# SwiGLU FFN of a two-layer decoder trunk: more products ahead of the operand combinations, and the last pair's two matrices in turns

## The chip, the cores and the metric

One Trainium2 chip, one core. The metric is the device time of one execution in microseconds, lower is better; for the kernel before it is the median of three runs.

## What is computed

A decoder trunk of two layers over 1024 tokens of width 1024, in float32. Layer 0 mixes tokens with stick-breaking and sliding-window attention, layer 1 with multi-head latent attention. Each layer ends in the part that the change touches, and both layers run it alike:

```python
def swiglu(h, w_gate, w_up, w_down):            # 1024 -> 2816 -> 1024
    return (jax.nn.silu(h @ w_gate) * (h @ w_up)) @ w_down

for layer in range(DEPTH):
    ...
    h = rmsnorm(x, ffn_norm[layer])
    x = x + swiglu(h, ffn_w_gate[layer], ffn_w_up[layer], ffn_w_down[layer])
return rmsnorm(x, final_norm)
```

## The kernel before

Activations lie transposed: a tile is 128 features by 512 tokens (half A or half B of the tokens). Every float32 operand is split in two float32r parts: ACT rounds it to the high part, DVE subtracts to get the low part. `split_w` (lines 141 to 147) does it for weights (tiles whi, wlo), `split` (lines 914 to 916) for activations. `mm3` (lines 228 to 232) then makes three matmuls: high by high, high weight by low activation, low weight by high activation.

The FFN (`ffn`, line 918) multiplies blocks two by two in Winograd's way: seven products in place of eight. The hidden width is taken as 11 pairs of 128-wide blocks. For each pair and for each of the two matrices (gate, g = 0; up, g = 1) there are seven products, named after the activation operand that they use, the *form*: B11, B21, T2, T1, T3, B22, N4. A form is four tiles (k = 0 to 3), each split in high and low. One product is 12 matmuls of 128x512 on PE. Four PSUM names take turns for the results (mm, a, b, d). On the weight side a matrix is loaded as four blocks (wa, wa, wb, wb); POOL makes three sums and differences of them and a fourth later (`combine` and `prep` in `forms`, lines 171 to 224). `take` prepares weights four products ahead of the one that is issued.

The FFN has three stages:

- **The head.** Forms B11 and B21 need half A alone, which is normalised first. So for the first NA = 4 pairs the products B11 and B21 of both matrices come first (16 products, lines 996 to 1014); their sums are written to DRAM (`keep`) and fetched again later. Meanwhile `combinations(k)` (line 984) makes the five other forms from half B: two normalised tiles (h_tile, line 950), one DVE and three POOL subtractions, five splits. It is called once at the end of each of the four pairs, for k = 0 to 3.
- **The pairs.** For each of the 11 pairs gate, then up: the remaining five products for the first four pairs (weights of kind "rest", which need all four POOL operations before their first product), all seven for the others (kind "fast", whose first two products need none). DVE adds the products up, ACT applies SiLU to gate, DVE multiplies by it, and `combine` (line 959) makes the four combined operands for the down projection on POOL. All go to DRAM. In layer 0 POOL also computes rotary tables in this stage (`rope_tables`), one step after each product.
- **Down.** The down projection takes the pairs in chunks of 4, 4 and 3. Its seven forms for a chunk are fetched from DRAM and split by `build` (line 1061) into the same tiles that the forms of the stage before used, so a tile can be written only when its last product has read it. For the first chunk the 28 tiles are fetched through a ring of three tiles named lone, after all pairs; for the next chunks, form by form behind the products of the last column of the chunk before.

Each engine has one queue that runs in order. The order in it is laid out at build time by a scheduler that follows the program's order and its own estimate of when each operand is ready.

Of the kernel before, what the change touches and what calls it, by code (L numbers as in the profile page):

```python
# [10 lines left out]
F32 = mybir.dt.float32  # L11
# [3 lines left out]
AF = mybir.ActivationFunctionType  # L15
ALU = mybir.AluOpType
# [55 lines left out]
class Kernel:  # L72
# [98 lines left out]
    def forms(self, mats):  # L171
# [7 lines left out]
        flat = [(i, j) for i, m in enumerate(mats) for j in range(len(turns.get(m[0], m[1])))]  # L179
        raws, ready = {}, []  # L180

        def load(i):
# [6 lines left out]
            if kind != "plain":  # L189
                t.append(self.tl(self.wx, [P, HALF], F32, "s1"))  # L190
# [8 lines left out]
        def prep():  # L199
            i, j = flat[len(ready)]  # L200
            kind, _, n = mats[i]
            if j == 0:
                for x in (i, i + 1):
                    if x < len(mats) and x not in raws:
                        load(x)
# [712 lines left out]
    def ffn(self, layer, xt, rs, accs, first, last):  # L918
# [13 lines left out]
        NA = 4  # L932
# [14 lines left out]
        take = self.forms(mats)  # L947
# [48 lines left out]
        tb = ExitStack()  # L996
        for i in range(NA):
            for g in range(2):
# [14 lines left out]
                elif g == 1:  # L1013
                    combinations(i)
# [3 lines left out]
        with self.pool("tc", side="right") as self.tp:  # L1018
            t = lambda tag: self.tl(self.tp, [P, HALF], F32, tag)
            for i in range(NP):  # L1020
# [3 lines left out]
                for g in range(2):  # L1024

                    def done(x, key, name=None):
                        if g == 0:
                            nc.scalar.activation(x, x, AF.Silu)
                            sil[key] = x
                        else:  # L1030
                            nc.vector.tensor_tensor(x, x, sil[key], ALU.mult)  # L1031
                            if name:
                                keep(x, name, i)

                    u, c11 = t(f"u{g}"), t(f"c11{g}")
                    if i < NA:
                        fetch(u, f"U{g}", i)
                        if g == 0:
                            sil[0] = c11
                        else:  # L1040
                            fetch(c11, "B11", i)
                    else:
                        nc.scalar.copy(u, p("B11"))
                        add(c11, u, p("B21"))
                        done(c11, 0, "B11")
                    add(u, u, p("T2"))
                    p5, c12, c22 = p("T1"), t(f"c12{g}"), t(f"c22{g}")
                    add(c12, u, p5)
                    add(u, u, p("T3"))
                    add(c22, u, p5)  # L1050
                    done(c22, 1, "B22")
                    add(c12, c12, p("B22"))
                    done(c12, 2)
                    add(u, u, p("N4"))
                    done(u, 3, "B21")
                combine(i, c11, c12, u, c22, sil[0], sil[2], sil[1])
            for _ in side:
                pass
# [7 lines left out]
            for name in FORMS:  # L1066
                build(name, *chunks[0], (self.rp, [P, HALF], F32, "lone", 3))
# [604 lines left out]
```

## Time and profile before

| | |
|---|---|
| time, median of 3 runs (lowest to highest) | 2510.03 us (2509.27 to 2511.41) |
| time of the profiled execution | 2502.03 us |
| its span, first to last instruction | 2500.3 us |
| PE busy (matmul) | 2334.6 us, 93% |
| DVE busy | 1912.7 us, 77% |
| ACT busy | 1237.0 us, 49% |
| POOL busy | 979.4 us, 39% |
| mean granted TensorE clock | 0.972 |
| HBM traffic | 115 GB/s over the span |

The busy shares are averages over stages with different limits. Views by stretch, engine by engine, tell more: a view of windows gives for each stretch the busy time and number of instructions of each engine, and a timeline lists instructions with the idle time ahead of each and what ended it.

### The profile page before, as it was taken

The page shows a single profiled execution, that of the slowest core. Times are in us where ns is not written, and L with a number is a line of the kernel's source. Part 1 is how long each engine was busy: PE and PEld are TensorE (multiplying, and loading weights), DVE is VectorE, ACT ScalarE, POOL GpSimd, SP SyncE. Part 2 cuts the span into 40 slices and gives each one's busy share as a digit, 9 for nine tenths or more (in the row PEclk, how much of TensorE's full clock was granted, in tenths as well). Part 3 has the DMA queues.
Part 4 walks back from the last instruction along what each step waited for, and adds up shares of the span by engine and source line. Part 5 has one row for each costly group of instructions (what it writes and reads, how often), then busy time and mean ns, then how long its engine had stood idle before and what let it go on. Part 6 is the DMA issues. An engine that isn't in the chain of part 4 may idle for free. (4 is left out here: it accounts for less than half of the span.)

```text
span 2500.3 us, 33743 instructions
## 1 busy us (share of the span) xinstructions
PE 2334.6 (93%) x11252; PEld 1913.9 (77%) x11252; DVE 1912.7 (77%) x2864; ACT 1237.0 (49%) x2469; POOL 979.4 (39%) x786
## 2 busy tenths in 40 slices
PE   7999999888999999899987999999989999998996
PEld 4777787776788888678766888887768888886784
DVE  6777776779676667799977888885588766678988
ACT  5555555554233334344655787774453333343453
POOL 5333232216975354343222323321047544533333
PEclk9999999999999999999998999999989999999998
DMA  3011225543444234453333111135225433345531
GB/s 119 26 43 39 68 99 192 189 171 122 141 137 140 88 107 151 145 171 123 121 115 95 50 62 60 53 133 195 90 96 183 146 105 102 107 129 170 169 103 71
DMA packets 161931, 289.22 MB, mean 116 GB/s; under 512 B 20091, under 2 KB 28764, under 8 KB 161756
## 3 DMA queue, kind: packets, MB, share of 16 engines
q1 hardware_dynamic: 161756, 287.05, 35.1%
q8 instruction: 89, 1.46, 0.2%
q14 instruction: 86, 0.70, 0.1%
HBM read 207.19 MB, written 79.27 MB: 115 GB/s over the span
## 5 line engine op out<-in xcount | busy, mean ns | idle before, releaser
L145 ACT CAST whi<-wa 128x512 fp32r<-128x512 f32 (+1 forms) x422 | 255.8, 607 | 473.3 <-PE mm L231 118.8
L146 DVE TENSOR_TENSOR wlo<-wa,whi 128x512 fp32r<-128x512 f32 (+1 forms) x422 | 334.0, 792 | 63.9 <-ACT whi L145 62.2
L177 POOL TENSOR_TENSOR wa<-s,wa 128x512 f32<-128x512 f32 (+1 forms) x68 | 97.0, 1426 | 327.1 <-DVE wlo L146 297.8
L195 POOL TENSOR_TENSOR s<-wb,wb 128x512 f32<-128x512 f32 (+1 forms) x68 | 104.6, 1538 | 161.6 <-DVE wlo L146 146.2
L146 DVE TENSOR_TENSOR wlo<-wb,whi 128x512 fp32r<-128x512 f32 (+1 forms) x136 | 136.2, 1001 | 33.3 <-ACT whi L145 33.2
L1424 PE MATMUL z<-mk,mq 128*128 128x512 f32 (+2 forms) x576 | 148.1, 369 | 11.2 <-ACT w L1437 10.4
L145 ACT CAST whi<-wb 128x512 fp32r<-128x512 f32 (+1 forms) x136 | 82.3, 605 | 142.3 <-PE a L231 43.6
L230 PE MATMUL mm<-hh,whi 128*128 128x512 f32 x312 | 129.0, 413 | 1.7 <-ACT whi L145 1.7
L1437 ACT ACTIVATE w<-z,st 128x512 f32<-128x512 f32 (+3 forms) x192 | 110.9, 583 | 35.3 <-DVE st L1433 25.4
L231 PE MATMUL mm<-hl,whi 128*128 128x512 f32 x312 | 125.6, 403 | 0.0
L177 POOL TENSOR_TENSOR wa<-wa,wa 128x512 f32<-128x512 f32 (+1 forms) x68 | 100.0, 1471 | 65.3 <-issue 52.0
L232 PE MATMUL mm<-hh,wlo 128*128 128x512 f32 x312 | 125.4, 402 | 0.0
L1430 DVE TENSOR_REDUCE st<-z 128x1 f32<-128x512 f32 (+1 forms) x192 | 104.2, 550 | 26.8 <-PE z L1424 19.1
L391 DVE TENSOR_TENSOR ptl<-t,pth 128x512 fp32r<-128x512 f32 x160 | 108.2, 684 | 18.2 <-ACT pth L390 13.5
L927 POOL TENSOR_TENSOR c<-c,c 128x512 f32<-128x512 f32 x66 | 99.3, 1518 | 43.1 <-DVE c L1031 37.1
L1424 PEld LDWEIGHTS z<-mk,mq 128*128 128x128 f32 x576 | 93.4, 194 | 24.7 <-ACT w L1437 16.2
L177 POOL TENSOR_TENSOR wb<-wa,wb 128x512 f32<-128x512 f32 (+1 forms) x68 | 101.9, 1499 | 3.5
L390 ACT CAST pth<-t 128x512 fp32r<-128x512 f32 x160 | 91.1, 590 | 19.0 <-PE t L387 8.0
L395 PE MATMUL mm<-pth,v 128*128 128x256 f32 x320 | 94.6, 312 | 2.9 <-ACT pth L390 2.8
L387 PE MATMUL t<-ident,w 128*128 128x128 f32 x576 | 94.8, 277 | 1.3 <-ACT w L1437 1.2
L395 PE MATMUL mm<-ptl,v 128*128 128x256 f32 x320 | 88.0, 299 | 2.0 <-DVE ptl L391 2.0
L703 DVE TENSOR_TENSOR ptl<-t,pth 128x512 fp32r<-128x512 f32 x80 | 54.4, 683 | 41.0 <-ACT pth L702 40.5
(526 smaller groups left out, 7640.4 us busy)
## 6 DMA issues: line engine op xcount, KB each, us to landing
a<-c SPq DMA_DIRECT2D x124, 256.0 KB, 2.1
ld<-a SPq DMA_DIRECT2D x98, 256.0 KB, 3.7
wa<-w_gate SPq DMA_DIRECT2D x60, 256.0 KB, 2.7
wa<-w_up SPq DMA_DIRECT2D x60, 256.0 KB, 2.6
lone<-a SPq DMA_DIRECT2D x56, 256.0 KB, 3.3
wb<-w_gate SPq DMA_DIRECT2D x44, 256.0 KB, 2.9
wb<-w_up SPq DMA_DIRECT2D x44, 256.0 KB, 2.8
wa<-w_in SPq DMA_DIRECT2D x36, 256.0 KB, 2.6
```

Source lines behind the costliest of these rows:

```text
L145: nc.scalar.copy(hi[:, :n], raw[:, :n])
L146: nc.vector.tensor_tensor(lo[:, :n], raw[:, :n], f(hi[:, :n]), ALU.subtract)
L177: sub = lambda o, x, y: nc.gpsimd.tensor_tensor(o, x, y, ALU.subtract)
L195: nc.gpsimd.tensor_tensor(s1, a21, a22, ALU.add)
L230: mm(ps, wh, xh, start=first, stop=False)
L231: mm(ps, wh, xl, start=False, stop=False)
L232: mm(ps, wl, xh, start=False, stop=last)
L391: nc.vector.tensor_tensor(lo, t, f(hi), ALU.subtract)
L395: nc.tensor.matmul(o[:, :256], vs, pt[:, j * 256:(j + 1) * 256], start=(kb == kb0 and j == 0 and i == 0), stop=(kb == NB - 2 and j == 1 an ...
L1424: nc.tensor.matmul(z[:, :wd + ext], qq[:, q0:q0 + P], kk[:, k0 - ext:k0 + wd], start=y == 0, stop=y == 2 and x > 0)
L1430: nc.vector.tensor_reduce(st[:, x:x + 1], zs[x], AX.X, ALU.max, negate=True)
L1437: nc.scalar.activation(w[:, o:o + wd], zs[x], AF.Exp, bias=st[:, 2 * np_ - 2:2 * np_ - 1], accum_out=box[p]["s"][c // 2][:, 8 * x + j:8 * ...
```

## The change

It changes `forms` and `ffn` in three ways.

1. NA goes from 4 to 6: the head has 24 products, and two more pairs have their B11 sums written to DRAM and fetched.
2. `combinations(k)` becomes a generator of five parts; the 20 parts of the four k are taken one after each product of the head, from the third product on.
3. In the last pair gate and up take turns form by form (`twins`), and the first down chunk's operands of a form are built as soon as both matrices have used that form. For this both matrices' weights are held at once; the one extra weight tile (s1) of the second is taken from the ring lone, which `build` also uses. The first down matrix is loaded at the second matrix's last form instead of its first.

The core of the diff (the body of `outputs` is the old code with a `yield` after each product, and is cut here):

```diff
-    def forms(self, mats):
+    def forms(self, mats, twins=None):
...
+        if twins is not None:
+            both = [x for x in flat if x[0] in twins]
+            at = flat.index(both[0])
+            flat[at:at + len(both)] = sorted(both, key=lambda x: (x[1], x[0]))
...
-                t.append(self.tl(self.wx, [P, HALF], F32, "s1"))
+                t.append(self.tl(self.rp, [P, HALF], F32, "lone", 3) if twins is not None and i == twins[1] else
+                         self.tl(self.wx, [P, HALF], F32, "s1"))
...
-            if j == 0:
+            early = twins is not None and i == twins[1]
+            if j == (6 if early else 0):
                 for x in (i, i + 1):
                     if x < len(mats) and x not in raws:
                         load(x)
...
-        NA = 4
+        NA = 6
...
-        take = self.forms(mats)
+        twins = (2 * NA + 2 * NP - 2, 2 * NA + 2 * NP - 1)
+        take = self.forms(mats, twins)
...
-            h12, h22 = h_tile(k, B, t()), h_tile(4 + k, B, t())
-            t1, t2, n4 = t(), t(), t()
+            h12 = h_tile(k, B, t())
+            t1 = t()
             sub(t1, h12, raw["B11"][k])
+            yield
+            h22 = h_tile(4 + k, B, t())
+            part("B22", h22)
+            yield
+            t2 = t()
             sub(t2, h22, t1)
             nc.vector.tensor_tensor(h12, h22, h12, ALU.subtract)
+            part("T1", t1)
+            yield
+            n4 = t()
             sub(n4, raw["B21"][k], t2)
-            for n, x in (("T2", t2), ("T1", t1), ("T3", h12), ("B22", h22), ("N4", n4)):
-                F[n][k] = self.form_tile(n, k)
-                self.split(x, F[n][k])
+            part("T2", t2)
+            yield
+            part("T3", h12)
+            part("N4", n4)
+            yield
...
-                elif g == 1:
-                    combinations(i)
+                    side = (x for k in range(4) for x in combinations(k))
+        for _ in side:
+            pass
...
+                gs = [outputs(i, g, sil) for g in range(2)]
+                if i < NP - 1:
+                    for g in gs:
+                        for _ in g:
+                            pass
+                else:
+                    for n, name in enumerate(FORMS):
+                        for g in gs:
+                            next(g, None)
+                        if n > 0:
+                            build(FORMS[n - 1], *chunks[0], ring)
...
-            for name in FORMS:
-                build(name, *chunks[0], (self.rp, [P, HALF], F32, "lone", 3))
+            build(FORMS[-1], *chunks[0], ring)
```

How the built order changes, at two places of DVE's queue. The first is the head of layer 0, from the low part of the weights of product 10 to that of product 11; hb are the tiles of half B from which the forms are made. Before:

```order
L146 TENSOR_TENSOR wlo_5893<-wa_5791,whi_5892 128x512
L990 TENSOR_TENSOR hb_5813<-hb_5815,hb_5813 128x512
L916 TENSOR_TENSOR B22l_5837<-hb_5815,B22h_5836 128x512
L916 TENSOR_TENSOR T1l_5829<-hb_5817,T1h_5828 128x512
L950 SCALAR_TENSOR_TENSOR hb_5936<-x_11344_5239,gains_66,rr_5750 128x512
L950 SCALAR_TENSOR_TENSOR hb_5938<-x_11348_5247,gains_66,rr_5750 128x512
L916 TENSOR_TENSOR T2l_5825<-hb_5818,T2h_5824 128x512
L916 TENSOR_TENSOR T3l_5833<-hb_5813,T3h_5832 128x512
L146 TENSOR_TENSOR wlo_5917<-wa_5867,whi_5916 128x512
```

Of the change, the same place:

```order
L146 TENSOR_TENSOR wlo_5885<-wa_5795,whi_5884 128x512
L1008 TENSOR_TENSOR hb_5785<-hb_5813,hb_5785 128x512
L923 TENSOR_TENSOR B22l_5816<-hb_5813,B22h_5815 128x512
L923 TENSOR_TENSOR T1l_5846<-hb_5787,T1h_5845 128x512
L958 SCALAR_TENSOR_TENSOR hb_5932<-x_11344_5239,gains_66,rr_5750 128x512
L923 TENSOR_TENSOR T2l_5876<-hb_5842,T2h_5875 128x512
L923 TENSOR_TENSOR T3l_5901<-hb_5785,T3h_5900 128x512
L146 TENSOR_TENSOR wlo_5917<-wa_5853,whi_5916 128x512
```

One normalised tile of seven instructions has moved from between the two weight splits to behind them. The second place is the end of the pairs in layer 0, where the first down operands (B11l) enter DVE's queue. Before, among the products of the last up matrix:

```order
L928 TENSOR_TENSOR u_9223<-u_9223,d_9352 128x512
L146 TENSOR_TENSOR wlo_9375<-s_9145,whi_9374 128x512
L916 TENSOR_TENSOR B11l_9538<-lone_9539,B11h_9537 128x512
L916 TENSOR_TENSOR B11l_9544<-lone_9545,B11h_9543 128x512
L916 TENSOR_TENSOR B11l_9550<-lone_9551,B11h_9549 128x512
L146 TENSOR_TENSOR wlo_9393<-wb_9141,whi_9392 128x512
L916 TENSOR_TENSOR B11l_9556<-lone_9557,B11h_9555 128x512
L928 TENSOR_TENSOR c_9372<-u_9371,a_9391 128x512
```

Of the change, after the second of the last pair's 14 products:

```order
L1052 TENSOR_TENSOR u_9095<-u_9095,u_8947 128x512
L146 TENSOR_TENSOR wlo_9289<-wa_9025,whi_9288 128x512
L923 TENSOR_TENSOR B11l_9346<-lone_9347,B11h_9345 128x512
L923 TENSOR_TENSOR B11l_9352<-lone_9353,B11h_9351 128x512
L146 TENSOR_TENSOR wlo_9307<-wa_9175,whi_9306 128x512
L935 TENSOR_TENSOR c_9262<-u_9261,d_9305 128x512
L923 TENSOR_TENSOR B11l_9358<-lone_9359,B11h_9357 128x512
L146 TENSOR_TENSOR wlo_9326<-s_9033,whi_9325 128x512
L923 TENSOR_TENSOR B11l_9364<-lone_9365,B11h_9363 128x512
```

The first B11l stood behind the last pair's eighth product (the first of its up matrix) and stands behind the second now, with splits of weights and sums of products between the builds.

## Rows read from the trace of the kernel before

**Rows 1.** Windows of the core: length, busy us and instructions per engine, granted clock, DMA

```profile
core 0: us, PE busy (x) PEld busy (x) DVE busy (x) ACT busy (x) POOL busy (x), PEclk, DMA share, GB/s
570.00:610.00 40.00, 30.51 (x112) 23.86 (x111) 38.85 (x43) 19.99 (x35) 27.58 (x15) 0.87 0.28 89
1840.00:1870.00 30.00, 21.84 (x74) 16.72 (x74) 28.85 (x31) 13.71 (x25) 23.01 (x12) 0.83 0.23 79
1000.00:1030.00 30.00, 23.56 (x72) 14.78 (x71) 23.39 (x31) 12.77 (x22) 11.15 (x8) 0.83 0.70 228
2250.00:2290.00 40.00, 32.91 (x122) 23.55 (x121) 34.69 (x46) 16.19 (x28) 15.91 (x10) 0.91 0.73 235
1880.00:1970.00 90.00, 90.00 (x399) 74.47 (x398) 72.54 (x85) 26.04 (x45) 60.01 (x41) 1.00 0.53 178
620.00:710.00 90.00, 86.68 (x372) 70.28 (x371) 58.64 (x74) 22.69 (x39) 86.56 (x102) 0.98 0.44 145
1832.90:1877.00 44.10, 35.94 (x135) 27.96 (x134) 42.95 (x49) 21.57 (x37) 30.69 (x16) 0.88 0.31 104
1375.00:1687.00 312.00, 305.62 (x2037) 262.19 (x2036) 259.48 (x513) 246.93 (x638) 101.75 (x79) 1.00 0.22 71
```

**Rows 2.** Timeline of PE, head of layer 1: start, duration, idle before and its end

```profile
1838.69 0.39 PE L230 MATMUL mm<-B21h,whi 128*128 128x512 f32 x1
...
1841.41 0.39 PE L230 MATMUL a<-B11h,whi 128*128 128x512 f32 x1
...
1846.44 0.79 PE L232 MATMUL a<-B11h,wlo 128*128 128x512 f32 x1 [4.41 <-DVE wlo L146]
...
1857.27 0.80 PE L230 MATMUL a<-B11h,whi 128*128 128x512 f32 x1 [3.08 <-ACT whi L145]
```

**Rows 3.** Timeline of DVE, the same stretch

```profile
1832.90 1.41 DVE L950 SCALAR_TENSOR_TENSOR hb<-x,gains,rr 128x512 f32<-128x512 f32 x2
...
1835.94 1.77 DVE L990 TENSOR_TENSOR hb<-hb,hb 128x512 f32<-128x512 f32 x1
...
1839.35 0.68 DVE L916 TENSOR_TENSOR T1l<-hb,T1h 128x512 fp32r<-128x512 f32 x1
...
1844.64 1.74 DVE L146 TENSOR_TENSOR wlo<-wa,whi 128x512 fp32r<-128x512 f32 x1
...
1876.28 0.69 DVE L916 TENSOR_TENSOR T3l<-hb,T3h 128x512 fp32r<-128x512 f32 x1
```

**Rows 4.** Timeline of POOL, the same stretch, and one operation after it

```profile
1835.54 1.62 POOL L927 TENSOR_TENSOR hb<-hb,hb 128x512 f32<-128x512 f32 x1
...
1850.80 5.25 POOL L927 TENSOR_TENSOR hb<-hb,T1l 128x512 f32<-128x512 f32 x1 [4.96 <-DVE hb L950]
...
1887.91 1.29 POOL L195 TENSOR_TENSOR s<-wb,wb 128x512 f32<-128x512 f32 x1 [4.05 <-DMA wb<-w_gate]
```

**Rows 5.** Timelines of PE and ACT, end of the pairs in layer 1: last pair, eighth product

```profile
2227.89 0.39 PE L230 MATMUL b<-B11h,whi 128*128 128x512 f32 x1
...
2228.77 0.62 ACT L915 CAST B11h<-lone 128x512 fp32r<-128x512 f32 x1 [0.23 <-PE b L232]
```

**Rows 6.** Timelines of PE and DVE, first down column of layer 1

```profile
2257.03 0.50 PE L232 MATMUL mm<-T1h,wlo 128*128 128x512 f32 x1 [1.33 <-DVE wlo L146]
2261.61 0.50 PE L231 MATMUL mm<-T1l,whi 128*128 128x512 f32 x1 [2.47 <-DVE T1l L916]
...
2279.74 1.02 DVE L916 TENSOR_TENSOR N4l<-lone,N4h 128x512 fp32r<-128x512 f32 x1 [0.67 <-ACT N4h L915]
```

**Rows 7.** Tile lone, 2225 to 2285: idle of its users, and its transfers

```profile
  DMA lone<-a: 25.6, 22
...
DMA to landing us min/median/max: 2.6/2.9/3.4
```

**Rows 8.** Timeline of PE, pairs of layer 0

```profile
678.35 0.50 PE L232 MATMUL b<-T2h,wlo 128*128 128x512 f32 x1 [2.08 <-DVE wlo L146]
```

More of the change, by code (lines that the diff above doesn't have):

```diff
@@ L1019, in ffn, with outputs, done, build @@
             t = lambda tag: self.tl(self.tp, [P, HALF], F32, tag)
+            def outputs(i, g, sil):
+                def done(x, key, name=None):
+                    if g == 0:
+                        nc.scalar.activation(x, x, AF.Silu)
+                        sil[key] = x
+                    else:
+                        nc.vector.tensor_tensor(x, x, sil[key], ALU.mult)
+                        if name:
+                            keep(x, name, i)
+                u, c11 = t(f"u{g}"), t(f"c11{g}")
+                if i < NA:
+                    fetch(u, f"U{g}", i)
+                    if g == 0:
+                        sil[0] = c11
+                    else:
+                        fetch(c11, "B11", i)
+                else:
+                    nc.scalar.copy(u, p("B11"))
+                    yield
+                    add(c11, u, p("B21"))
+                    done(c11, 0, "B11")
+                    yield
+                add(u, u, p("T2"))
+                yield
+                p5, c12, c22 = p("T1"), t(f"c12{g}"), t(f"c22{g}")
+                add(c12, u, p5)
+                yield
+                add(u, u, p("T3"))
+                add(c22, u, p5)
+                done(c22, 1, "B22")
+                yield
+                add(c12, c12, p("B22"))
+                done(c12, 2)
+                yield
+                add(u, u, p("N4"))
+                done(u, 3, "B21")
+                out[g] = c11, c12, u, c22
+            def build(name, p0, n, ring):
+                for k in range(n):
+                    F[name][k] = self.form_tile(name, k)
+                    self.split(fetch(self.tl(*ring), name, p0 + k), F[name][k])
+            out = {}
+            ring = (self.rp, [P, HALF], F32, "lone", 3)
             for i in range(NP):
@@ L1023, in ffn @@
                     side = self.rope_tables(self.tp)
[L1024 to L1055, printed above, removed]
+                gs = [outputs(i, g, sil) for g in range(2)]
[3 more added lines that the diff above has]
+                            pass
+                else:
+                    for n, name in enumerate(FORMS):
[3 more added lines that the diff above has]
+                            build(FORMS[n - 1], *chunks[0], ring)
+                c11, c12, u, c22 = out[1]
                 combine(i, c11, c12, u, c22, sil[0], sil[2], sil[1])
@@ L1058, in ffn @@
                 pass
-            def build(name, p0, n, ring):
-                for k in range(n):
-                    F[name][k] = self.form_tile(name, k)
-                    self.split(fetch(self.tl(*ring), name, p0 + k), F[name][k])
-            for name in FORMS:
-                build(name, *chunks[0], (self.rp, [P, HALF], F32, "lone", 3))
+            build(FORMS[-1], *chunks[0], ring)
         self.rctx.close()
```

3 lines of the change are left out of this document (added).

## The prediction, made before the change was timed

> **What bounds the kernel now.** I read the windows first, because the busy shares of the page mix stages. Where nothing holds PE up, in the pairs of layer 1, it is busy for the whole stretch at the full granted clock, and 399 matmuls are recorded in 90 us, 4.43 per us [rows 1]. That is the pace to hold other stretches against. Four stretches of the FFN fall short of it [rows 1]. The head of layer 0 has 112 matmuls in 40 us, where 177 would go: 65 missing, 14.7 us. The head of layer 1 has 74 in 30 us, where 133 would go: 13.3 us. The change-over from the pairs to the down projection has 72 in 30 us in layer 0 (13.8 us) and 122 in 40 us in layer 1 (12.5 us). Each sum holds the gaps and the matmuls at a lower granted clock behind them: 0.83 to 0.91 in these stretches, a mix of the 1.2 and 2.4 GHz levels. Together they are 54.3 us, 2.2% of the time: the most that this change can get there.
>
> Next the timelines of the queues. In the head PE waits 4.41 us for the low part of a weight (wlo, from DVE) and 3.08 us for a high part (whi, from ACT) [rows 2]. DVE is busy meanwhile: 42.95 of 44.1 us [rows 1]. Its queue holds form combinations between two weight splits, and some last long: a subtraction of two SBUF tiles takes 0.68 us [rows 3], but 1.77 us where POOL works on a subtraction of its own [rows 3, 4]. At the change-over PE waits for splits of down operands, T1l for instance, and of weights [rows 6]. The first of these operands is cast at 2228.77, right behind the read of the form that it overwrites; the last is split at 2280.76 [rows 5, 6]. ACT and DVE wait 25.6 us there for tiles of the ring lone to land [rows 7]. So the head is bound by DVE with POOL beside it, the change-over by a chain that starts late and passes through three buffers.
>
> **The change-over, step by step.** A product takes 2.72 us on PE (1838.69 to 1841.41) [rows 2]. The eighth product of the last pair starts at 2227.89 [rows 5]; the first started seven products earlier, at 2208.85. Today the first build waits for the eighth. With gate and up in turns it waits for the second, six products or 16.3 us earlier. The 28 builds take 52.0 us (2228.77 to 2280.76) [rows 5, 6], 1.86 us each. At this pace they would end at 2264.4. The last form, N4, is needed by the 21st product counted from the first of the last pair, which PE could start at 2263.25; its fourth tile is needed 2.0 us later, at 2265.3. So at the same pace nothing would be late. Against it: one of the three lone tiles holds the s1 of the second matrix until its fourth form is split, about the first four builds. A cycle of one tile takes 3 x 1.86 = 5.6 us today, so with two tiles these builds take 2.8 us each, 3.7 us more in all, and the last is some 2.8 us late. Also the splits of the first down column's weights stand between the last builds now, where POOL combines weights and stretches DVE as in the head. I leave 4 us lost at each change-over: a gain of 9.8 and 8.5 us, **18.3 us**. What is late next is the N4 form and the weight splits behind it. On SP the down weights now stand between the fetches of lone and wait for the same splits; their cover is the four products that weights are ahead, 10.9 us against a landing of 2.9 us [rows 7].
>
> **The head.** The work does not change, only its order: per k, eight DVE instructions and three POOL subtractions. The 20 parts are meant for 20 products. But the built order shows that DVE starts them as soon as their operands are ready: between the weight splits of products 10 and 11 stand six other instructions where there were seven. The 4.41 us gap is at product 11 [rows 2], so it stays but for 0.6 us. From the first normalised tile (1832.90) [rows 3] to the weight split of product 20 there are now 49 instructions on DVE. The window of the same length before also has 49: 42.95 us busy, where 49 at 0.60 us (a back-to-back pitch of the timeline, 1.41 us for two being 0.60 + 0.81) would be 29.4; the other 13.5 us are 0.85 us for each of POOL's 16 operations [rows 1, 3]. POOL has 12 in the new window. So the split is ready 29.4 + 12 x 0.85 = 39.6 us after 1832.90, or 42.5 us at the 1.09 us that the single row shows (1.77 less 0.68) [rows 3]: at 1872.5 to 1875.4. Product 11 began at 1841.41 [rows 2]; product 20 could begin nine products, 24.5 us, later, and takes its first low part 0.45 us into it: 1866.4. So 6 to 9 us are lost however well the rest goes, against 13.3 and 14.7. With matmuls at the lower clock behind the gaps I take 10 us as left in each head. The gain is 3.3 and 4.7 us, **8.0 us**. The last four products have no parts between them, so the rest of the weights has time, which it had not before.
>
> In a sentence of its own, the Trainium skill (SBUF — State Buffer, Who interferes with whom) says that a VectorE instruction with two SBUF inputs and a GpSimd instruction that reads SBUF exclude each other for a whole instruction. It speaks against spreading work that keeps both engines on SBUF: the collisions stay as many. By it the 12 operations would cost a whole POOL operation each, and the sum for the heads would be about nothing; rival 2 gives that case from rows alone. The trace agrees in one row, 1.77 us beside POOL's 1.62 [rows 3, 4], and shows the other side too: POOL needed 5.25 us once while DVE went on [rows 4].
>
> **What costs nothing, with its bounds.** Some 36 transfers of 256 KB are added (extra sums out and back, a first half of a weight loaded twice). In the pairs of layer 1, with the same kind of fetches, PE is never idle [rows 1], so 0; were one uncovered in each of four added pair stages, 4 x 2.9 = 12 us [rows 7]. In layer 0 POOL is 96% busy for 90 us while the rotary tables are made, and PE has 372 matmuls instead of 399 there, 6.1 us lost [rows 1]. These 90 us are 33 products; they lay in the eight "rest" matrices and lie in the first of twelve now. I take 0, with bounds of 6.1 us gained (the head leaves POOL free earlier) and four more gaps of 2.08 us [rows 8], 8 us lost. The attention of layer 1 is not edited, but a few of its matmuls change places in the built order; PE is idle there for 6.4 of 312 us [rows 1], so I take 0 and bound it by 6.4 us on either side.
>
> **The sum.** The profiled execution took 2502.03 us (span 2500.3). Less 18.3 and 8.0 it is 2475.7. The median of the runs stands 8.0 us above the profiled execution, so I forecast **2484 us**, a gain of 1.0%.
>
> **Rivals.**
> 1. *Both places clear up.* If POOL's operations fall beside DVE instructions that read PSUM, DVE is no longer the bound in the head; it would lose some 2.5 us in each. That is 15 us more: 2469. For it: POOL took the waiting once [rows 4]. Against: the built order bunches the parts. Chance 0.14.
> 2. *The heads gain nothing, the change does there what it did before.* If a POOL operation costs DVE its own 1.29 us [rows 4], the split of product 20 is ready at 1832.90 + 29.4 + 15.5 = 1877.8, 11.4 us late, and with the slow matmuls nothing is left. 2510.0 - 18.3: 2492. Chance 0.20.
> 3. *The change-overs gain nothing.* If builds take some 2.3 us each, as splits, sums and casts now wait in the same queues behind late tiles, they end 12 us after their time, as today. Only the heads count: 2502. Chance 0.10.
> 4. *Slower: the ring lone starves.* If s1 keeps its tile in effect throughout, or the in-order queues make two tiles of three, a build takes 5.6 / 2 = 2.8 us; 28 of them from 2212.3 end at 2290, 25 us after their time. Two change-overs lose 50 where they lose 26.3: 24 us more, less 8 of the heads, 2526. It decides against the change from 2.4 us per build on, and PE would wait in the last pair already. For it: 25.6 us of waiting for lone [rows 7]. Against: the s1 is read for the last time within the first few builds in the built order. Chance 0.06.
>
> **How the numbers follow.** The forecast has 0.48 and its own range is 2476 to 2492; some 0.02 is left for what I don't see. The range takes in rivals 1 and 2, most of 3, and the unknown costs: 2468 to 2503, leaving out rival 4, the far end of rival 1 and a part of 3. About 0.2%, 5 us, is what a measurement of this kernel can tell from no change. Faster by more: the forecast, rivals 1 and 2 and half of 3, 0.86. Within: the other half and remainders, 0.07. Slower: 0.07.
>
> **What would show it.** In the changed profile the last pair's builds should start behind its second product, with PE gaps of under 4 us in the first down column, and none in the last pair. In the heads a gap of about 4 us should stand at product 11 as before, then several of 0.5 to 2 us up to product 20, and DVE should stay busy until its last combination, about 43 us after the first. Wrong would be: heads without gaps, gaps ahead of the twelfth product of the last pair, or a change in a stage that isn't edited.

## The result, and the profile after the change

The changed kernel took 2476.67 us (median of 4 runs, 2473.04 to 2484.19), the kernel before 2509.65 us (4 runs): a ratio of 0.9872, with a 95% interval of 0.9848 to 0.9897. The forecast was 2484 us in a range of 2468 to 2503, so time, range and sign held. The terms behind it did not all hold, and they are what the experiments are about.

To see where the time went I use one measure for every kernel below. A product that nothing holds up takes 2.72 us from its first matmul to the first of the next; what it takes above that is its **loss**, with the wait and the slower matmuls behind it. The products come in the same number and at the same ordinal place in all kernels, so losses can be summed by stage (where the matmuls of neighbours mix, each twelve in PE's order count as one product): the head (products 11 to 24), the rest stage of layer 0 (25 to 60), the change-over (146 to 170).

| us lost | head, layer 0 / 1 | rest stage, layer 0 | change-over, layer 0 / 1 |
|---|---|---|---|
| before | 14.9 / 13.8 | 6.3 | 14.6 / 12.9 |
| forecast for the change | 10 / 10 | as before | 4 / 4 |
| changed | 9.4 / 8.2 | 7.4 | 6.1 / 6.6 |

From their first product to the 201st the two FFNs are 12.3 and 10.4 us shorter (591.4 to 579.1, 580.0 to 569.6). The spans differ by 24.2 us (2500.3 and 2476.1). What is left comes from stages without an edit: from the 201st product of layer 0 to the first of layer 1 it is 670.9 us, where it was 675.2, and up to the first product of layer 0 543.2, where it was 540.3. In the twelve profiles of the experiments below these two stretches vary from 669.9 to 676.2 and from 538.7 to 544.5, so neither difference can be put down to the change.

Windows of the changed kernel, lengths and columns as in [rows 1] (heads of layer 0 and 1, change-overs, pairs of layer 1):

```profile
573.00:613.00 40.00, 34.07 (x137) 25.93 (x136) 40.00 (x49) 22.61 (x40) 16.48 (x11) 0.96 0.34 117
1828.00:1858.00 30.00, 23.81 (x98) 17.73 (x98) 30.00 (x36) 15.83 (x29) 16.04 (x9) 1.00 0.38 125
990.00:1020.00 30.00, 25.89 (x108) 19.89 (x108) 27.91 (x36) 13.78 (x25) 15.80 (x10) 1.00 0.73 230
2222.00:2262.00 40.00, 35.75 (x151) 27.73 (x152) 38.04 (x52) 19.15 (x34) 16.05 (x11) 1.00 0.74 227
1870.00:1960.00 90.00, 90.00 (x398) 74.51 (x397) 70.80 (x82) 27.68 (x47) 57.50 (x40) 1.00 0.45 150
```

The heads have 137 and 98 matmuls where [rows 1] has 112 and 74, the change-overs 108 and 151 where it has 72 and 122. DVE is busy for the whole of both head windows, and the granted clock there is 0.96 and 1.00 instead of 0.87 and 0.83. The pairs are as they were.

PE's timeline in the head of layer 1: the first matmul of product 11, its wait, the first matmul of product 12, and the three longest waits after that (the idle time in brackets, and what ended it):

```profile
1829.19 0.39 PE L237 MATMUL a<-B11h,whi 128*128 128x512 f32 x1
...
1831.41 0.50 PE L239 MATMUL a<-B11h,wlo 128*128 128x512 f32 x1 [1.60 <-DVE wlo L146]
...
1833.84 0.39 PE L237 MATMUL b<-B21h,whi 128*128 128x512 f32 x1
...
1839.15 0.50 PE L239 MATMUL d<-B11h,wlo 128*128 128x512 f32 x1 [1.73 <-DVE wlo L146]
...
1843.28 0.50 PE L237 MATMUL a<-B11h,whi 128*128 128x512 f32 x1 [1.07 <-ACT whi L145]
...
1853.29 0.50 PE L239 MATMUL d<-B11h,wlo 128*128 128x512 f32 x1 [1.56 <-DVE wlo L146]
```

Product 11 lasts 4.65 us and loses 1.93. Before, its wait alone was 4.41 us and the matmul behind it took 0.79 [rows 2], and it lost 6.25. The work is pulled apart: no wait is over 1.8 us, and the clock stays up.

DVE's queue between the weight splits of products 10 and 11, with one split further on, and POOL beside it:

```profile
1822.60 1.18 DVE L146 TENSOR_TENSOR wlo<-wa,whi 128x512 fp32r<-128x512 f32 x1
1823.71 1.77 DVE L1008 TENSOR_TENSOR hb<-hb,hb 128x512 f32<-128x512 f32 x1
1825.41 1.79 DVE L923 TENSOR_TENSOR B22l<-hb,B22h 128x512 fp32r<-128x512 f32 x1
1827.12 0.68 DVE L923 TENSOR_TENSOR T1l<-hb,T1h 128x512 fp32r<-128x512 f32 x1
...
1828.38 0.68 DVE L923 TENSOR_TENSOR T3l<-hb,T3h 128x512 fp32r<-128x512 f32 x1
1828.98 1.77 DVE L923 TENSOR_TENSOR T2l<-hb,T2h 128x512 fp32r<-128x512 f32 x1
1830.67 0.68 DVE L146 TENSOR_TENSOR wlo<-wa,whi 128x512 fp32r<-128x512 f32 x1
...
1839.02 0.68 DVE L923 TENSOR_TENSOR T2l<-hb,T2h 128x512 fp32r<-128x512 f32 x1
```

```profile
1823.31 1.62 POOL L934 TENSOR_TENSOR hb<-hb,hb 128x512 f32<-128x512 f32 x1
1825.01 1.63 POOL L934 TENSOR_TENSOR hb<-N4l,hb 128x512 f32<-128x512 f32 x1
1828.54 1.67 POOL L934 TENSOR_TENSOR hb<-hb,T1l 128x512 f32<-128x512 f32 x1 [1.89 <-DVE hb L958]
1832.18 1.60 POOL L934 TENSOR_TENSOR hb<-hb,hb 128x512 f32<-128x512 f32 x1 [1.98 <-DVE hb L958]
...
1838.63 3.42 POOL L934 TENSOR_TENSOR hb<-hb,T1l 128x512 f32<-128x512 f32 x1 [3.16 <-DVE hb L958]
...
1854.67 1.29 POOL L934 TENSOR_TENSOR hb<-hb,hb 128x512 f32<-128x512 f32 x1 [3.18 <-DVE hb L958]
```

From split to split it is 8.07 us with six instructions between, three of them stretched to 1.77 us or more, each beside a POOL operation. The kernel before has 9.81 us there (1834.83 to 1844.64), with seven instructions and four of them stretched, and the split itself takes 1.74 [rows 3]. Two of its rows:

```profile
1834.83 1.19 DVE L146 TENSOR_TENSOR wlo<-wa,whi 128x512 fp32r<-128x512 f32 x1
...
1841.28 1.77 DVE L916 TENSOR_TENSOR T3l<-hb,T3h 128x512 fp32r<-128x512 f32 x1
```

So the wait at product 11 is 2.8 us shorter for two reasons: one normalised tile less between the splits, some 0.7 us, and two stretches less, those of T3l and of the split, some 2.1 us.

From the first half-B tile (1820.68) to the last combination (1863.03) DVE's timeline has 51 instructions, 12 of them stretched by 11.1 us in all, for 12 POOL operations: 0.92 us each.

In the first down column of layer 1 PE waits for weight splits too, and no longer for a down operand, as it did in [rows 6]. PE's timeline, its three longest waits there:

```profile
2231.19 0.50 PE L239 MATMUL a<-B11h,wlo 128*128 128x512 f32 x1 [0.68 <-DVE wlo L146]
2238.10 0.50 PE L239 MATMUL d<-T2h,wlo 128*128 128x512 f32 x1 [1.17 <-DVE wlo L146]
2246.08 0.50 PE L239 MATMUL a<-T3h,wlo 128*128 128x512 f32 x1 [1.53 <-DVE wlo L146]
```

The first cast of the 28 builds and the high part of the weight that PE waits for at 2246.08 (ACT's timeline), the low part of that weight and the last split (DVE's), and a piece of what POOL does in between (three subtractions of the last pair's results, 5.05 us):

```profile
2196.14 1.14 ACT L922 CAST B11h<-lone 128x512 fp32r<-128x512 f32 x2
...
2239.51 0.61 ACT L145 CAST whi<-wb 128x512 fp32r<-128x512 f32 x1
```

```profile
2244.28 1.75 DVE L146 TENSOR_TENSOR wlo<-wb,whi 128x512 fp32r<-128x512 f32 x1
...
2251.96 0.69 DVE L923 TENSOR_TENSOR N4l<-lone,N4h 128x512 fp32r<-128x512 f32 x1 [1.84 <-ACT N4h L922]
```

```profile
2235.83 5.05 POOL L934 TENSOR_TENSOR c<-c,c 128x512 f32<-128x512 f32 x3 [0.63 <-DVE c L1052]
```

The builds begin behind the second product of the last pair, as forecast, and take 56.5 us (52.0 before; the sum with two tiles of lone had 55.7). The weight of the longest wait had its high part at 2240.12, and DVE came to its low part 4.2 us later: what PE waits for there is DVE's queue, and not POOL's sum, which was ready.

### The profile page after: what moved, and what is told of

Same layout as the page of the kernel before. It is cut to its first block, busy times and chain, and to the rows that moved or that the text cites. A ratio compares the mean times of both kernels' runs of the same rounds, so it can differ in the third digit from the quotient of the medians.

```text
span 2476.1 us, 33778 instructions
## 1 busy us (share of the span) xinstructions
PE 2320.3 (94%) x11252; PEld 1907.3 (77%) x11252; DVE 1914.9 (77%) x2864; ACT 1232.4 (50%) x2469; POOL 970.2 (39%) x786
## 3 DMA queue, kind: packets, MB, share of 16 engines
q1 hardware_dynamic: 166940, 296.49, 36.7%
## 5 line engine op out<-in xcount | busy, mean ns | idle before, releaser
L146 DVE TENSOR_TENSOR wlo<-wa,whi 128x512 fp32r<-128x512 f32 (+1 forms) x422 | 343.2, 814 | 75.4 <-ACT whi L145 73.5
L201 POOL TENSOR_TENSOR s<-wb,wb 128x512 f32<-128x512 f32 (+1 forms) x66 | 93.6, 1418 | 203.9 <-DVE wlo L146 149.9
L178 POOL TENSOR_TENSOR wa<-wa,wa 128x512 f32<-128x512 f32 (+1 forms) x68 | 105.3, 1549 | 43.9 <-issue 26.8
L398 DVE TENSOR_TENSOR ptl<-t,pth 128x512 fp32r<-128x512 f32 x160 | 108.0, 682 | 13.3 <-ACT pth L397 10.7
L934 POOL TENSOR_TENSOR c<-c,c 128x512 f32<-128x512 f32 x66 | 101.6, 1554 | 26.0 <-DVE c L1052 22.7
L1470 PEld LDWEIGHTS z<-mk,mq 128*128 128x128 f32 x576 | 93.6, 193 | 23.3 <-ACT w L1483 14.6
```

Of the source, the lines that this page charges most:

```text
L146: nc.vector.tensor_tensor(lo[:, :n], raw[:, :n], f(hi[:, :n]), ALU.subtract)
L178: sub = lambda o, x, y: nc.gpsimd.tensor_tensor(o, x, y, ALU.subtract)
L398: nc.vector.tensor_tensor(lo, t, f(hi), ALU.subtract)
L934: sub = lambda o, x, y: nc.gpsimd.tensor_tensor(o, x, y, ALU.subtract)
L1470: nc.tensor.matmul(z[:, :wd + ext], qq[:, q0:q0 + P], kk[:, k0 - ext:k0 + wd], start=y == 0, stop=y == 2 and x > 0)
```

## The experiments

All of them in one table, by the same measure. Where the code is the same, a head or a change-over of one layer differs by up to 1.9 us from kernel to kernel, so less than that is not read. The ratios are to the kernel before, timed on the same chip.

| edit | head 0 / 1 | rest 0 | change-over 0 / 1 | median us | ratio (95%) |
|---|---|---|---|---|---|
| last pair only | 13.6 / 13.9 | 8.6 | 6.4 / 6.5 | 2491.58 | 0.9937 (0.9920 to 0.9954) |
| head only | 8.0 / 8.2 | 9.9 | 13.0 / 13.0 | 2495.75 | 0.9956 (0.9940 to 0.9971) |
| six pairs, blocks | 10.8 / 11.2 | 7.1 | 14.1 / 14.3 | 2500.27 | 0.9968 (0.9953 to 0.9983) |
| four pairs, 20 parts | 17.7 / 16.6 | 7.1 | 14.5 / 14.3 | 2511.30 | 1.0020 (1.0001 to 1.0039) |
| combinations on DVE | 0.2 / 0.4 | 8.9 | 7.7 / 4.7 | 2467.76 | 0.9852 (0.9818 to 0.9886) |
| s1 in ring rr | 8.1 / 8.2 | 8.4 | 5.2 / 5.4 | 2477.83 | 0.9885 (0.9862 to 0.9908) |
| five tiles for builds | 8.0 / 8.2 | 7.9 | 6.0 / 5.0 | 2477.77 | 0.9886 (0.9866 to 0.9906) |
| eight pairs, parts later | 8.6 / 8.8 | 6.0 | 6.4 / 5.4 | 2475.49 | 0.9878 (0.9858 to 0.9898) |
| change-over sums on DVE | 8.6 / 8.2 | 9.2 | 1.6 / 1.7 | 2472.80 | 0.9865 (0.9848 to 0.9881) |
| all FFN sums on DVE | 0.0 / 0.0 | 0.6 | 0.0 / 0.4 | 2439.95 | 0.9732 (0.9717 to 0.9746) |
| three of these edits | 0.1 / 0.4 | 9.3 | 0.0 / 0.5 | 2451.63 | 0.9782 (0.9767 to 0.9796) |
| before, all sums on DVE | 6.3 / 5.9 | 0.0 | 9.8 / 10.8 | 2473.56 | 0.9872 (0.9847 to 0.9898) |

### One part of the change at a time

Last pair only: the changed kernel with `NA = 4` and the old `combinations`.

```diff
-        NA = 6
+        NA = 4
-                    side = (x for k in range(4) for x in combinations(k))
+                elif g == 1 and i < 4:
+                    combinations(i)
```

> Only the last pair by turns, with the builds behind; four pairs ahead and the combinations in four blocks as before. If the two parts of the change add up (the theory), the change-overs lose 6.1 and 6.6 us as in the changed kernel and the heads some 14 us each as in the kernel before: 14.7 us less than before, a ratio of 0.994 (0.993 to 0.996). Rival, the parts need each other (the builds came earlier only because the transfers and sums of the stages before them had moved): the change-overs gain less than 7 us in all and the ratio is over 0.997.

Head only: `twins` is not given, all pairs run one matrix after the other, and the builds stand behind them.

```diff
-        take = self.forms(mats, twins)
+        take = self.forms(mats)
-                if i < NP - 1:
+                if i < NP:
-            build(FORMS[-1], *chunks[0], ring)
+            for name in FORMS:
+                build(name, *chunks[0], ring)
```

> Only the head: six pairs ahead and the combinations in 20 parts; the last pair and the builds as before. If the parts add up, the heads lose 9.4 and 8.2 us as in the changed kernel, the rest stage of layer 0 about 1.7 us more than before, the change-overs 13.8 and 12.5 us as before: 8 us less than before in all, a ratio of 0.997 (0.996 to 0.998). Rival: the heads were only better in the changed kernel's one profile; then they lose 13 us or more here and the ratio is 0.999 to 1.001.

Both theories held in place: each part gains in its own stage and leaves the other stage as it was. In size the first held; the head alone came out at 0.9956, a little past its range of 0.996 to 0.998, with 3.6 us more lost in the rest stage where 1.7 were expected. The two FFNs are 10.7 us shorter with the first part, 9.4 with the second, 22.7 with both, so the parts add up to within 3 us; in time 0.63% and 0.44% stand against 1.28%, which the intervals allow.

### The two halves of the head's edit

Six pairs with the combinations in the old four blocks; then four pairs with the 20 parts, the last six of them drained behind the head. Neither has the turns.

```diff
-                    side = (x for k in range(4) for x in combinations(k))
+                elif g == 1 and i < 4:
+                    combinations(i)
```

```diff
-        NA = 6
+        NA = 4
```

> Six pairs ahead, but the combinations in four blocks behind products 4, 8, 12 and 16 as before, and no turns in the last pair. Theory of the prediction (DVE takes the combinations when their operands are ready, the places in the program count for little): heads lose 9 to 10 us each as with the 20 parts, the gap at product 11 is under 2 us, ratio 0.997. Rival, the parts do it: the heads lose 13 to 15 us each as before, with over 4 us at product 11 and 3 us at product 13, and the ratio is 0.999 to 1.002.

> The combinations in 20 parts, but four pairs ahead as before, so that the last parts come behind the last of these products, and no turns in the last pair. Theory of the prediction (what counts is how many products the work of DVE has to lie beside): heads lose 13 to 15 us each, ratio 0.999 to 1.001. Rival, the parts do it: heads lose 8 to 10 us each, ratio 0.997.

PE's two longest waits in the head of layer 1, with six pairs and blocks:

```profile
1849.31 0.79 PE L239 MATMUL a<-B11h,wlo 128*128 128x512 f32 x1 [4.39 <-DVE wlo L146]
1860.14 0.50 PE L237 MATMUL a<-B11h,whi 128*128 128x512 f32 x1 [2.37 <-ACT whi L145]
```

and with four pairs and 20 parts, the wait at product 11 and the two longest:

```profile
1846.66 0.50 PE L239 MATMUL a<-B11h,wlo 128*128 128x512 f32 x1 [1.60 <-DVE wlo L146]
...
1871.17 0.50 PE L239 MATMUL d<-T2h,wlo 128*128 128x512 f32 x1 [1.76 <-DVE wlo L146]
1880.91 0.79 PE L239 MATMUL a<-T3h,wlo 128*128 128x512 f32 x1 [3.97 <-DVE wlo L146]
```

Both of my theories fell in part. The gap at product 11 shrinks with the parts (1.60 us even with four pairs) and stays with the blocks (4.39 us even with six): the grouping does count, and the prediction said that it would not. POOL's and DVE's timelines show how, with six pairs and blocks:

```profile
1845.45 1.59 POOL L934 TENSOR_TENSOR hb<-hb,hb 128x512 f32<-128x512 f32 x1
1847.12 1.59 POOL L934 TENSOR_TENSOR hb<-N4l,hb 128x512 f32<-128x512 f32 x1
```

```profile
1847.51 1.75 DVE L146 TENSOR_TENSOR wlo<-wa,whi 128x512 fp32r<-128x512 f32 x1
```

In a block both normalised tiles of a k come together, so POOL's three subtractions run in a row, and the last stretches the split that product 11 waits for. With the parts the second tile stands behind this split, POOL waits 1.98 us for it (1832.18 in the changed kernel), and the split takes 0.68.

But with four pairs the work that the parts take out of product 11 comes back at products 17 to 19, where the forms are wanted, and the kernel is no faster, by its interval a little slower. The two edits need each other: six pairs alone take 4.1 and 2.6 us off the heads, the parts on top of them 2.8 and 3.0.

### The ring at the change-over

First s1 of the last up matrix in a tile of rr (idle since the head); then, with s1 in lone, every other build in a tile of rr.

```diff
-                t.append(self.tl(self.rp, [P, HALF], F32, "lone", 3) if twins is not None and i == twins[1] else
+                t.append(self.tl(self.rp, [P, HALF], F32, "rr", 2) if twins is not None and i == twins[1] else
```

```diff
-                    self.split(fetch(self.tl(*ring), name, p0 + k), F[name][k])
+                    tag = ring if ring[2:] != (F32, "lone", 3) or k % 2 == 0 else (self.rp, [P, HALF], F32, "rr", 2)
+                    self.split(fetch(self.tl(*tag), name, p0 + k), F[name][k])
```

> The changed kernel with the sum s1 of the last up matrix in a tile of the ring rr, which is free by then, so that the builds have all three tiles of lone. Theory of the prediction (what is left at the change-overs is the late start of the first builds with two tiles): 2 to 4 us less lost in each, 2 to 4 in place of 6.1 and 6.6. Rival (what is left is the weight splits that wait in DVE's queue behind splits, sums and stretched instructions, however early the builds began): under 1 us less in each.

> The changed kernel with every other build of the first chunk in a tile of the ring rr, so that five tiles serve the builds and s1. If a ring is what holds the builds (ACT waits over 22 us for tiles of lone to land in each change-over), this frees all of it: that waiting falls under 8 us, and the change-overs lose 1 to 3 us each where they lost 6.1 and 6.6. Rival (DVE's queue is what is left): the waiting for lone falls just so, but the change-overs still lose over 5 us each.

Idle time before users of lone until a tile landed, 2185 to 2265 (us, times), in the changed kernel, with s1 in rr, and with five tiles:

```profile
  DMA lone<-a: 23.3, 18
```

```profile
  DMA lone<-a: 17.5, 16
```

```profile
  DMA lone<-a: 0.9, 1
```

With five tiles the waiting for lone is all but gone (10.2 us for rr come in), and PE's longest wait there is no shorter, 2.18 us for a weight split:

```profile
2241.14 0.50 PE L239 MATMUL mm<-T1h,wlo 128*128 128x512 f32 x1 [2.18 <-DVE wlo L146]
```

The rival holds in the main: the change-overs lose 5.0 to 6.0 us either way, at most 1.7 less than in the changed kernel and within what the same code varies by (it had said under 1 us less, and still over 5 with five tiles). Most of what is left is not the ring's.

### Eight pairs ahead, the parts later

```diff
-        NA = 6
+        NA = 8
+                if i == 1 and g == 1:
                     side = (x for k in range(4) for x in combinations(k))
```

> The changed kernel with eight pairs ahead and the 20 parts behind products 8 to 27 in place of 2 to 21. The factors of the second token half come only about 27 us into the FFN, at product 9, so the first seven parts are overdue there and bunch. Theory (the heads lose what DVE's bunch lasts longer than the products beside it): with 20 products for the 20 parts the heads lose 2 to 5 us each where they lost 9.4 and 8.2. Rival (DVE's order is set by readiness, not by the place in the program): the bunch comes at products 11 to 18 as before and the heads lose 8 to 10 us. Four more matrices of the kind rest stand beside the rotary tables in layer 0, which may cost up to 6 us there.

The rival holds: 8.6 and 8.8 us, at the same products 11, 13 and 17 as in the changed kernel. Six products later in the program, the parts stand at the same time on DVE (the last split of a form 69.6 us after the first product of layer 1, 69.1 in the changed kernel), and two more pairs ahead bring nothing.

### The combinations' subtractions on DVE

```diff
-            sub(t1, h12, raw["B11"][k])
+            dsub(t1, h12, raw["B11"][k])
```

`dsub` is the same subtraction on nc.vector; t2 and n4 are made with it too.

> The changed kernel with the three subtractions per k of the combinations on DVE in place of POOL; nothing else. Theory (in the heads DVE is the bound, and each POOL subtraction beside it costs it some 0.85 us in stretched instructions): DVE gains 12 instructions of 0.60 us, 7.2 us, and loses 12 x 0.85 us, 10.2 us, of stretching; the heads lose 5 to 7 us each where they lost 9.4 and 8.2, and no instruction of the combinations lasts over 1.3 us. Rival 1, DVE is the bound but the stretching is not POOL's doing: 7 us more in each head, 15 to 17. Rival 2, the skill's rule in full (one whole POOL operation of 1.3 us or more for each): heads lose 0 to 2 us.

The heads lose 0.2 and 0.4 us. DVE between the weight splits of products 10 and 11 of layer 1, and a window of the head:

```profile
1821.35 0.68 DVE L146 TENSOR_TENSOR wlo<-wa,whi 128x512 fp32r<-128x512 f32 x1
1821.95 0.68 DVE L992 TENSOR_TENSOR hb<-hb,hb 128x512 f32<-128x512 f32 x1
...
1825.62 0.68 DVE L146 TENSOR_TENSOR wlo<-wa,whi 128x512 fp32r<-128x512 f32 x1
```

```profile
1825.00:1855.00 30.00, 30.00 (x134) 24.86 (x133) 30.00 (x51) 18.36 (x33) 0.00 (x0) 1.00 0.50 165
```

Six instructions stand between the two splits again, two of them subtractions that were POOL's (two splits of forms have moved behind), and it is 4.27 us from split to split in place of 8.07. DVE has twelve instructions more and is faster: 63 in 38.6 us from 1818.69 on, none stretched, where the changed kernel had 51 in 42.4. PE has no gap left. My own figure (5 to 7 us) was too careful; rival 2's range, 0 to 2, holds, but not its reason, since a POOL operation cost DVE 0.92 us, less than its own 1.29. DVE saves 11.1 - 7.2 = 3.9 us, and PE 8 to 9: the weight splits come when they are wanted, while the combinations end some 3 us later in the FFN than in the changed kernel (72.0 us after its first product, 69.1 there). The heads gain 17.0 us over the changed kernel, but the two FFNs 13.6: in layer 0 some of it is lost again in stages whose code is the same. The built order moved as well; how much of the rest is the order's and how much the stretches' was not separated.

The Trainium skill (SBUF — State Buffer, Who interferes with whom) says that a VectorE instruction with two inputs in SBUF and a GpSimd instruction that reads SBUF exclude each other, and that whichever comes first makes the other wait. The trace agrees that either can wait: DVE at 1.77 beside POOL's 1.62 to 1.67, and POOL at 3.42 where DVE went on. It does not agree on the order there: by the profile's starts POOL's operation came first (1838.63), and DVE splits that started behind it (1839.02) took their 0.68 us. By that rule the prediction's rival 2 saw no gain in spreading. The measured heads gained 11.1 us, with the collisions still there.

### The change-over's sums on DVE, and all of them

First the sums of the first two down matrices and the last pair's results; then the sums of all weights and all results, and the combinations. In both, `sub` and the sum in `combine` take their engine from `eng`.

```diff
+        eng = lambda: nc.vector if twins is not None and cur[0] in (twins[1] + 1, twins[1] + 2) else nc.gpsimd
-            nc.gpsimd.tensor_tensor(s1, a21, a22, ALU.add)
+            eng().tensor_tensor(s1, a21, a22, ALU.add)
...
+            e = nc.vector if pair == NP - 1 else nc.gpsimd
+            for o, y, z in ((t1, a12, a11), (a12, a22, a12), (t2, a22, t1), (n4, a21, t2)):
+                e.tensor_tensor(o, y, z, ALU.subtract)
```

For all sums on DVE, `eng` and `e` are nc.vector for every weight and every pair, and the combinations use `dsub`. The third run joins the first of these two edits, `dsub`, and s1 in rr.

> The changed kernel with the sums of the first two down matrices and the four subtractions of the last pair's results on DVE in place of POOL: 12 operations that lie beside the builds and the first down products. Theory, after the heads (what is left at the change-overs is DVE stretched by POOL): 12 x 0.60 us more for DVE against some 10.6 us of stretching that go; the change-overs lose 1 to 4 us each where they lost 6.1 and 6.6. Rival (the queue of DVE is too long there with or without POOL): they lose 5 to 9 us each.

> All of the FFN's subtractions and sums of two SBUF tiles on DVE: the combinations, the sums of all weights and the results of all pairs; POOL keeps the rotary tables and what lies outside the FFN. Theory (beside POOL two-SBUF instructions of DVE stretch, and that costs DVE more than the work itself would): in the pairs of layer 1 DVE, 70.8 us busy in 90 with 82 instructions beside 40 of POOL, takes some 122 x 0.61 = 74 us and PE stays without a gap; the heads lose under 1 us, the rest stage of layer 0 under 5 us (7.4 in the changed kernel), the change-overs 0 to 3 us each; 15 to 25 us less than the changed kernel. Rival (DVE becomes the bound over long stretches): PE loses 10 us or more in the pairs, and the kernel is no faster than the changed one.

> The changed kernel with three edits: the combinations' subtractions on DVE, those of the change-over on DVE, and s1 of the last up matrix in the ring rr. If the effects add up: heads lose under 1 us each, change-overs 0 to 4 us each, 17 to 27 us less than the changed kernel. Rival: the change-overs stay at 5 us or more, and it stands where the combinations alone on DVE stood, some 10 us under the changed kernel.

A window of the change-over of layer 1 with its sums on DVE, and its one wait of PE over 0.2 us:

```profile
2215.00:2255.00 40.00, 38.85 (x171) 31.52 (x169) 37.35 (x59) 19.79 (x35) 2.91 (x2) 1.00 0.73 234
```

```profile
2241.72 0.50 PE L239 MATMUL d<-N4h,whi 128*128 128x512 f32 x1 [1.15 <-ACT N4h L924]
```

Change-overs lose 1.6 and 1.7 us where they lost 6.1 and 6.6: what the change left there was DVE stretched by POOL. The wait that remains is for a build; in the run of three edits, with s1 in rr, it is gone and the change-overs lose 0.0 and 0.5. So the ring may matter once DVE is out of the way, but only 1.2 to 1.6 us, less than the same code varies by. From the first to the 201st product the two FFNs of that run are 25.3 us shorter than the changed kernel's, where the three edits alone give 13.6 (combinations), 8.8 (change-over) and 1.4 (s1): they add up, as expected.

With all sums on DVE, the change-over and the pairs of layer 1:

```profile
2185.00:2235.00 50.00, 49.94 (x221) 41.04 (x220) 48.82 (x82) 23.39 (x41) 0.00 (x0) 1.00 0.69 217
1850.00:1940.00 90.00, 90.00 (x399) 74.55 (x398) 75.03 (x123) 26.43 (x44) 0.00 (x0) 1.00 0.46 160
```

In the pairs DVE takes on 41 instructions, from 82 to 123 in 90 us, for 4.2 us more busy time, 70.80 to 75.03. PE stays without a gap. The rest stage of layer 0, where POOL also makes the rotary tables, loses 0.6 us instead of 7.4. The kernel takes 2439.95 us, 2.7% less than before and 36.7 us under the changed kernel's median (33.9 when each is held against the kernel before on its own chip). Its FFNs are 38.7 us shorter than the changed kernel's: 17.6 in the heads, 12.3 at the change-overs, 6.8 in the rest stage, by the table's losses. I had expected 15 to 25 in all, less than the same theory gave stage by stage.

### Is the change still worth anything then?

The kernel before, with the same edit in `forms` and in `ffn`:

```diff
-        sub = lambda o, x, y: nc.gpsimd.tensor_tensor(o, x, y, ALU.subtract)
+        sub = lambda o, x, y: nc.vector.tensor_tensor(o, x, y, ALU.subtract)
-            nc.gpsimd.tensor_tensor(s1, a21, a22, ALU.add)
+            nc.vector.tensor_tensor(s1, a21, a22, ALU.add)
```

> The kernel before (four pairs ahead, combinations in blocks, the last pair's matrices one after the other, builds behind the eighth product) with all subtractions and sums of two SBUF tiles of the FFN on DVE, as in the run before of the changed kernel. Theory (what the change spreads is real work of DVE that the old order does not leave room for, stretched or not): the heads lose 4 to 10 us each, the change-overs 4 to 12 us each, and this kernel stands 15 to 35 us above the changed kernel with the same edit, at some 2455 to 2475 us. Rival (the change only treated the stretching): heads and change-overs lose under 2 us each, and it stands within 5 us of the changed kernel with the same edit, at 2440 to 2446.

It takes 2473.56 us, 33.6 more than the changed kernel with the same edit. Heads lose 6.3 and 5.9 us, change-overs 9.8 and 10.8. In the head of layer 1 PE now waits for the forms and their weights once the sixteen products are used up:

```profile
1837.91 0.50 PE L233 MATMUL d<-T2h,wlo 128*128 128x512 f32 x1 [1.63 <-DVE wlo L146]
...
1847.72 0.50 PE L231 MATMUL d<-N4h,whi 128*128 128x512 f32 x1 [0.53 <-ACT whi L145]
```

So the theory holds: the order of the change is worth no less where POOL is out of the way, 33.6 us between the medians beside 33.0 with POOL. From the first to the 201st product the two FFNs differ by 32.1 us, beside 22.7.

## Why the prediction was right, and where it was not

That the sum came out is in part luck: the change-overs gave 3.5 us less than forecast, the heads 3.1 more, and the two misses cancel.

- **The change-over.** Right in mechanism: the builds start behind the second product instead of the eighth, and the run with the last pair alone shows the gain in this stage alone. The size was off: 14.8 us gained where 18.3 were forecast (8.5 and 6.3 for 9.8 and 8.5). The term that was mis-sized is "I leave 4 us lost at each change-over"; it measured 6.1 and 6.6. The text gave two reasons for what is left: one tile of lone is taken, and POOL stretches DVE among the last builds. It sized the first (2.8 us) and gave the second no price. With POOL there, freeing the ring gave 0.1 to 1.7 us; taking POOL's sums away gave 4.5 and 4.9.
- **The head.** The sum was nearly right, its inside wrong. 10 us were to be left in each, and 9.4 and 8.2 were: 11.1 us gained for 8.0. But the step "the 4.41 us gap is at product 11, so it stays but for 0.6 us" failed: the wait is 1.60 us. I counted the instructions between two splits (seven, now six) and not how many of them meet a POOL operation (four and the split, now three), which is where their length comes from; and I added slow matmuls behind gaps, while with gaps under 1.8 us the granted clock stayed at 1.00 in layer 1 (0.96 in layer 0). That six pairs alone would do it failed too: they give 6.7 of these 11 us, and the parts the rest.
- **The price of POOL.** 0.85 us per operation was worked out from the old head, 0.92 measured in the new one. The bound by DVE with POOL beside it was right: in layer 1 the split of product 20 was ready 41.2 us after the first half-B tile, between the 39.6 and 42.5 of the sum, and product 20 was 8.2 us late, between its 6 and 9. The run that removes POOL shows the bound directly. What I did not draw from it is that the work costs DVE less when DVE does it.
- **The rest stage and the transfers.** Taken as 0 with 6.1 us of gain and 8 of loss as bounds: 1.1 us more lost in layer 0, no gap in the pairs of layer 1. That fits, but the stage varies from 6.0 to 9.9 us among the kernels that keep POOL's sums, so the 36 added transfers were not weighed by themselves.
- **The rivals.** The ring as a brake (rival 4) did not come; PE lost 0.74 us at one product of the last pair. Both places clear (rival 1) did not come either: the heads kept 9.4 and 8.2 us, not 2.5. Rival 2 had the heads gain nothing, rival 3 the change-overs: the two single-part runs exclude both. (The chances given for "faster by more" add up to 0.87, not 0.86.)
- **The profiled execution and the median.** The sum was made against 2502.03 us and moved by 8.0 to the median. Before, the profiled execution stood 8.0 us under the median; after the change it stands 1.2 above (2477.88 beside 2476.67). So 26.3 us were forecast, 24.2 came between the profiled spans and 33.0 between the medians. Held against the profiled execution the sum is 2.2 us too low (2475.7), so that the forecast lies 7 us too high is this step alone: it takes the spread from run to run (2494 to 2517 us in 35 later runs of the kernel before) for a difference that stays.

## What to carry to other kernels

Take losses product by product, against the pace of a stage that nothing holds up: which edit acts where is then seen to a microsecond or two, also where the total cannot tell. Where DVE sets the pace, look at what POOL does beside it before spreading DVE's work over more time: in 90 us of the pairs, DVE was only 4.2 us longer busy when it made 41 operations of POOL's itself, and moving all such work gained as much again as the change. Then measure the old order again with that removed; here it showed that the new order still matters as much.

## What the runs showed of the hardware

- A subtraction of two 128x512 SBUF tiles lasts 0.68 us on DVE when POOL is still (0.60 from start to start), and up to 1.79 beside a POOL subtraction in the head of layer 1; POOL takes 1.29 alone [rows 4] and in that head 1.59 to 1.67 beside DVE, 3.42 once. A whole stage with POOL at work on such sums, 57.5 of 90 us, held DVE busy for 70.80 us with 82 instructions, and 123 without POOL took 75.03.
- The granted clock was 1.00 in a stretch of 30 us with PE waits of 1.60, 1.73, 1.07 and 1.56 us, and 0.83 in one with 4.41 and 3.08. The second pair of waits is also longer in sum (7.5 us beside 6.0), so what the length of a single wait does by itself is not shown.
